# Chunk scan of a gated hybrid block: the preparation of chunk n+1 written ahead of the products of chunk n

## The chip, the cores and the metric

The kernel runs on one core of one Trainium2 chip. Its metric is the device time of one execution in microseconds (us). Three executions of the kernel before took 2009.08, 2011.65 and 2013.90 us; the median is 2011.65 us. The core has a matrix engine (TensorE, PE in the profile, with its weight loads as PEld), a vector engine (DVE), an activation engine (ACT), GpSimd (POOL) and SyncE (SP), which here issues nearly all DMAs. Each engine works off its own instructions in the order in which they stand in the program, and waits at an instruction whose operands are not ready.

## The reference, cut to what matters

The program is one layer of a token mixer with three branches (an S5 scan, a Mamba-2 scan, an RG-LRU), merged by gates, and then an expert-choice mixture of experts. The change lies in the Mamba-2 branch. The sequence of 1024 tokens is cut into 8 chunks of 128; there are 4 groups of 4 heads each, and both directions are computed:

```
a_cum  = cumsum(a)                                   # per chunk and head
cb     = einsum('bcqgn,bcsgn->bgcqs', cm, bm)        # C times B, within a chunk
lmat   = exp(segsum(a))                              # decays within a chunk
y_diag = einsum('bgjcqs,bcsgjp->bcqgjp', cb * lmat, xs)
y_off  = einsum('bcqgn,bcgjpn->bcqgjp', cm, entering) * exp(a_cum)
y      = (y_diag + y_off + D * x) * silu(z)
```

`entering` is the state that enters a chunk; it is there before this stage begins.

## The kernel before, in words

The scan stage treats 32 chunks, group g (0 to 3) by chunk c (0 to 7); "chunk (1,0)" below is group 1, chunk 0, and tiles carry both digits (`rowb10`). `chunk(g, c)` does this for one of them:

- three loads issued by SP: `xe` (inputs and entering states, L790), `bc` (B and C, L792) and `rowb` (decay exponents of 4 heads in 2 directions, 128x1024, L795). Each of the three has 3 buffers, so a load for chunk n+3 waits until chunk n's tile has been read for the last time;
- the decays: ACT makes `dec = exp(rowb)` (two instructions of 64x512, L798; `dec` has 2 buffers); PE multiplies B by C into `pcb` (L800); DVE subtracts and clips `rowb` in place (L802, L803, 128x1024 each), ACT takes the exponential (L804), DVE adds the two directions (L805) and multiplies by `pcb` (L806). POOL multiplies `dec` by C (L807). What is ready for PE at the end is `rowb` by L806 and `dec` by L807;
- the products: 16 small matmuls on PE (L816 with `rowb`, L817 with `dec`) into two PSUM banks `yps`, which collect four chunks;
- after chunks 3 and 7 of a group, DVE adds D*x and multiplies by the gate z (L826, L827), ACT squares (L829, L831), POOL sums the squares (L832), and the result goes out (L833).

Two other works are woven into the same stretch. The RG-LRU branch, four tiles by two directions, has gate products on PE (`lps`, L887), tanh, exp and square root on ACT (L888 to L895) and products and scans on DVE (L894 to L908); a list, `LST`, says after which chunk a piece of it is written. And 24 tasks `gt` project the merge gates: 48 matmuls of 128x512 each on PE (L263 to L265), with a weight split (ACT L125, DVE L126) and an evacuation on ACT (L781). The gate tasks depend on nothing in the scan; they stand behind it in the program.

A scheduler sets the order on each engine from the order in which the program is written and from its own model of durations, so that gate matmuls fill in between the products of the chunks. `bank` gives one of 5 PSUM banks, used by `pcb`, `yps` and `lps` alike. Square root and the exponential are in different activation tables, so that ACT reloads a table before and after each L895.

The loop of the stage calls `chunk(g, c)` for all 32, with pieces of the RG-LRU and of the z projection between them.

Of the kernel before, what the change touches and what calls it, by code (L numbers as in the profile page):

```python
# [62 lines left out]
def backbone(ctx: ExitStack, tc: tile.TileContext, I, out, dbg=None, stop=None):  # L63
# [19 lines left out]
    def bank(name):  # L83
        return bankh[0](name)
# [599 lines left out]
    with tc.tile_pool(name="p2", bufs=1, reuse_waits="tile") as p2:  # L684
# [85 lines left out]
        def z_task(t):  # L770
            def ev(ps, t0, n):
                zt = zp.tile([P, 512], F32, tag="zt", name=f"zt{t}{t0}", bufs=3)
                A.activation(zt, ps, AF.Tanh, scale=0.5)
                V.scalar_tensor_tensor(zt, zt, 1.0, ps, op0=ALU.add, op1=ALU.mult)
                Y.dma_start(szd[t // 2][:, t % 2, t0:t0 + n], zt)
            proj(OFF_Z + t * P, P, False, f"z{t}", ev)
# [7 lines left out]

        yps = {}

        def chunk(g, c):
            q0 = c * P
            xe = p2.tile([P, 512], F32, tag="xe", name=f"xe{g}{c}", bufs=3)
            Y.dma_start(xe, xed[c][:, g, :])  # L790
# [3 lines left out]
            rowb = p2.tile([P, 2, 4, P], F32, tag="rowb", name=f"rowb{g}{c}", bufs=3)  # L794
            Y.dma_start(rowb.rearrange("p d h q -> p (d h q)"), dap(rowsd, (8 * g + c) * 8 * P, [[0, P], [1, 8 * P]]))  # L795
            dec = p2.tile([P, 4, P], F32, tag="dec", name=f"dec{g}{c}", bufs=2)
# [8 lines left out]
            V.tensor_add(rowb[:, 0], rowb[:, 0], rowb[:, 1])  # L805
            V.tensor_mul(rowb[:, 0], rowb[:, 0], pcb[:, None, 0:P].to_broadcast([P, 4, P]))  # L806
            G.tensor_mul(dec, dec, Cd[:, None, :].to_broadcast([P, 4, P]))  # L807
            if c % 4 == 0:
                for t in range(2):
                    yps[t] = bank(f"yps{g}{c}{t}")  # L810
# [100 lines left out]

        zs = [lambda t=t: z_task(t) for t in range(2, 8)]
        lrus = (s_ for t in range(4) for s_ in lru_tile(t))
        for g in range(4):
            for c in range(8):
                chunk(g, c)
                if c in (1, 4) and zs:
                    zs.pop(0)()
                for _ in range(LST[8 * g + c]):
                    next(lrus, None)  # L920
# [661 lines left out]
def build(inputs, dbg=None, stop=None):  # L1582
    import numpy as np
    import concourse.bacc as bacc
    nc = bacc.Bacc("TRN2", target_bir_lowering=False, num_devices=1)
    arrays, I = {}, {}
    for name in _INS:
        a = np.ascontiguousarray(inputs[name])
        arrays[f"in_{name}_dram"] = a
        I[name] = nc.dram_tensor(f"in_{name}_dram", a.shape, mybir.dt.from_np(a.dtype), kind="ExternalInput").ap()  # L1590
    out = nc.dram_tensor("out_0_dram", (1, S, D), F32, kind="ExternalOutput").ap()
    with tile.TileContext(nc, schedule_with_timeline_sim=True) as tc:
        backbone(tc, I, out, dbg=dbg, stop=stop)
    return nc, arrays
# [7 lines left out]
```

## Time and profile before

| what | value |
|---|---|
| profiled execution | 2013.96 us |
| its span on the core | 2012.2 us, so 1.8 us lie around it |
| median of three other runs | 2011.65 us (2009.08 to 2013.90) |
| PE busy over the span | 1873.0 us, 93% |
| DVE busy | 1586.2 us, 79% |
| ACT busy | 1020.2 us, 51% |
| POOL busy | 497.3 us, 25% |
| products of the chunks | from 647.3 to 958 us of the span |

The span has stages with different limits. The scan of the chunks is the stretch from 647.3 to 958 us; behind it PE goes on with the rest of the gate tasks, then with the output projections of the branches and the experts. A time in the profile is counted from the start of the span. The windows of the first group of rows below are cut where the products of chunks (0,0), (1,0), (2,0), (3,0) and (3,7) begin. "Idle before" in a row is the time in which the engine stood still just before the instructions of that row; the name behind the arrow is what ended it, and "issue" stands where the profile names nobody.

### The profile page before, as it was taken

What the parts mean: (1) busy time and instruction counts of PE and PEld (TensorE: products, weight loads), DVE (VectorE), ACT (ScalarE), POOL (GpSimd) and SP (SyncE); (2) the same over time, 40 slices, a digit from 0 to 9 for tenths busy, and PEclk for the clock granted to TensorE, in tenths of its full rate; (3) what the DMA queues carried; (4) which work ended last, traced back from release to release, by engine and by line L of the source; (5) the groups of instructions that cost most, each with busy time, mean ns of one, the idle gap of its engine ahead of it and who ended that gap; (6) DMA issues with size and microseconds to landing.
All of it is one profiled execution on the core that took longest, in us unless ns stands there. A gap on an engine that the chain in (4) does not pass through costs nothing.

```text
span 2012.2 us, 26882 instructions
## 1 busy us (share of the span) xinstructions
PE 1873.0 (93%) x9514; PEld 1503.9 (75%) x9514; DVE 1586.2 (79%) x2183; ACT 1020.2 (51%) x1313; POOL 497.3 (25%) x456
## 2 busy tenths in 40 slices
PE   5989999999899999899999999994699999999997
PEld 2668788887667777677887778773588888888885
DVE  4797778777464788888358855599799999999998
ACT  4533434432322766666421222322488878878785
POOL 1463343340143144332000001246201111010142
PEclk8989999999999999999999999997799999999999
DMA  9234334422677666664578853755799999999974
GB/s 328 36 96 116 103 104 117 120 85 83 189 243 213 193 213 213 217 220 155 185 244 315 279 172 131 258 181 188 260 349 405 390 397 391 401 394 392 375 280 166
DMA packets 273127, 462.64 MB, mean 230 GB/s; under 512 B 39968, under 2 KB 167632, under 8 KB 271968
## 3 DMA queue, kind: packets, MB, share of 16 engines
q1 hardware_dynamic: 268672, 445.19, 63.7%
q0 software_dynamic: 4320, 15.73, 3.0%
q8 instruction: 75, 1.23, 0.2%
q14 instruction: 60, 0.49, 0.1%
HBM read 384.44 MB, written 78.51 MB: 230 GB/s over the span
## 4 chain that ended last, share of the span: by engine, by line
PE 57%; DVE 8%; DMA 5%; issue 3%; ACT 2%; SPq 1%; POOL 1%; DVEq 0%; ACTq 0%; POOLq 0%
PE h_w L1482 6%; PE h_w L1483 6%; PE h_w L1484 6%; PE pj_gt L263 3%; PE pj_gt L265 3%; PE pj_gt L264 3%; PE py_w L1482 3%; PE py_w L1484 3%; PE py_w L1483 3%; PE wo L1299 2%; PE st L754 2%; DMA wm<-in_w_mod_dram 2%; PE bom L264 1%; PE bom L263 1%; PE bom L265 1%
## 5 line engine op out<-in xcount | busy, mean ns | idle before, releaser
L1377 DVE TENSOR_TENSOR el_w<-er_w,eh_w 128x1024 fp32r<-128x1024 f32 x384 | 460.0, 1221 | 25.2 <-ACT eh_w L1376 12.1
L1376 ACT CAST eh_w<-er_w 128x1024 fp32r<-128x1024 f32 x384 | 403.5, 1052 | 106.4 <-PE h_w L1483 66.3
L1482 PE MATMUL h_w<-eh_w,thi_x 128*128 128x512 f32 x512 | 203.5, 397 | 0.0
L1483 PE MATMUL h_w<-eh_w,tlo_x 128*128 128x512 f32 x512 | 200.6, 392 | 0.0
L1484 PE MATMUL h_w<-el_w,thi_x 128*128 128x512 f32 x512 | 200.5, 392 | 0.0
L265 PE MATMUL pj_gt<-hxh,wlo_gt 128*128 128x512 f32 x384 | 153.3, 399 | 0.0
L263 PE MATMUL pj_gt<-hxh,whi_gt 128*128 128x512 f32 x384 | 152.7, 398 | 0.0
L264 PE MATMUL pj_gt<-hxl,whi_gt 128*128 128x512 f32 x384 | 152.6, 397 | 0.0
L1484 PEld LDWEIGHTS h_w<-el_w,thi_x 128*128 128x128 f32 x512 | 96.6, 189 | 20.8 <-DVE el_w L1377 0.2
L1482 PEld LDWEIGHTS h_w<-eh_w,thi_x 128*128 128x128 f32 x512 | 96.7, 189 | 19.6 <-ACT thi_x L1400 0.2
L1483 PEld LDWEIGHTS h_w<-eh_w,tlo_x 128*128 128x128 f32 x512 | 96.7, 189 | 19.6 <-DVE tlo_x L1401 0.4
L1385 POOL DMA_INDIRECT xs<-h2d,idx x16 | 24.0, 1498 | 294.8 <-PE tb_x L1393 273.8
L1482 PE MATMUL py_w<-eh_w,thi_h 128*128 128x512 f32 x240 | 96.4, 402 | 0.0
L1483 PE MATMUL py_w<-eh_w,tlo_h 128*128 128x512 f32 x240 | 93.9, 391 | 0.0
L1484 PE MATMUL py_w<-el_w,thi_h 128*128 128x512 f32 x240 | 93.9, 391 | 0.0
L1418 POOL DMA_INDIRECT accd<-ysm,idx x14 | 49.6, 3545 | 149.5 <-DVE ysm L1416 138.9
L265 PEld LDWEIGHTS pj_gt<-hxh,wlo_gt 128*128 128x128 f32 x384 | 73.3, 191 | 16.8 <-issue 0.8
L263 PEld LDWEIGHTS pj_gt<-hxh,whi_gt 128*128 128x128 f32 x384 | 73.6, 192 | 16.2 <-issue 0.3
L264 PEld LDWEIGHTS pj_gt<-hxl,whi_gt 128*128 128x128 f32 x384 | 73.3, 191 | 16.0 <-issue 0.2
L807 POOL TENSOR_TENSOR dec<-dec,bc 128x512 f32<-128x512 f32 x32 | 61.8, 1935 | 88.8 <-ACT dec L798 88.7
L1207 POOL TENSOR_TENSOR r_wo<-r_wo,bc_m 128x1024 f32<-128x1024 f32 x4 | 10.2, 2558 | 272.4 <-DMA mgm<-mgd 139.4
L265 PE MATMUL pj_xb<-hxh,wlo_xb 128*128 128x512 f32 x192 | 76.8, 400 | 0.5 <-DVE wlo_xb L126 0.5
(650 smaller groups left out, 5013.0 us busy)
## 6 DMA issues: line engine op xcount, KB each, us to landing
er_w<-in_moe_w_dram SPq DMA_DIRECT2D x384, 512.0 KB
rowb<-rowsd SPq DMA_DIRECT2D x32, 512.0 KB
wm<-in_w_mod_dram SPq DMA_DIRECT2D x32, 512.0 KB
raw_gt<-in_w_in_dram SPq DMA_DIRECT2D x24, 512.0 KB
gtd<-gz SPq DMA_DIRECT2D x48, 256.0 KB
xk<-xed SPq DMA_DIRECT2D x18, 512.0 KB
wm<-in_w_mod_dram SPq DMA_DIRECT2D x8, 1024.0 KB
xe<-xed SPq DMA_DIRECT2D x32, 256.0 KB
```

The lines of the kernel that those rows point to most:

```text
L263: T.matmul(ps, wh(k), xh(k), start=(first and k == 0), stop=False)
L264: T.matmul(ps, wh(k), xl(k), start=False, stop=False)
L265: T.matmul(ps, wl(k), xh(k), start=False, stop=(last and k == nk - 1))
L754: T.matmul(st[g // 2][64 * d:64 * d + 64, (g % 2) * 256:(g % 2 + 1) * 256], xk[:, D + 64 * g:D + 64 * g + 64], xd[:, 256 * g:256 * g + 256 ...
L807: G.tensor_mul(dec, dec, Cd[:, None, :].to_broadcast([P, 4, P]))
L1299: T.matmul(st4[i]["ps"][n], ms[i][a][:, k], wo[k][b][:, sl], start=(k == 0 and q == 0), stop=(k == KC - 1 and q == 2))
L1376: A.copy(a, raw)
L1377: V.tensor_sub(b, raw, a.bitcast(F32))
L1418: G.indirect_dma_start(out=accd[:, :], out_offset=bass.IndirectOffsetOnAxis(ap=idx[:, e:e + 1], axis=0), in_=yss[e], in_offset=None, compu ...
L1482: T.matmul(ps[n], xa[:, j, :], a[:, sl], start=(j == 0), stop=False)
L1483: T.matmul(ps[n], xb[:, j, :], a[:, sl], start=False, stop=False)
L1484: T.matmul(ps[n], xa[:, j, :], b[:, sl], start=False, stop=(j == KC - 1))
```

## The change

`chunk(g, c)` is cut in two. `prep(g, c)` holds the loads, the decays and the product of B and C, up to L807, and returns the three tiles. `fin(g, c, ...)` holds the products and what follows them. The loop calls `prep` of the next chunk and then `fin` of the present one; `prep(0, 0)` stands ahead of the loop. No instruction is added or removed, and no buffer count changes.

```
-        def chunk(g, c):
+        def prep(g, c):
             q0 = c * P
             xe = p2.tile([P, 512], F32, tag="xe", name=f"xe{g}{c}", bufs=3)
...
             G.tensor_mul(dec, dec, Cd[:, None, :].to_broadcast([P, 4, P]))
+            return xe, rowb, dec
+
+        def fin(g, c, xe, rowb, dec):
             if c % 4 == 0:
...
+        nxt = prep(0, 0)
         for g in range(4):
             for c in range(8):
-                chunk(g, c)
+                cur, nxt = nxt, (prep(*divmod(8 * g + c + 1, 8)) if 8 * g + c < 31 else None)
+                fin(g, c, *cur)
```

Lines of the new program from `fin` on have numbers higher by 3 (L816 becomes L819, L887 becomes L890, and so on). What the scheduler makes of it is shown at three places; names are those of the tiles, with the two digits of group and chunk (or, for the RG-LRU, the tile `lq1`).

On DVE, between the end of the preparation of chunk (1,7) and that of chunk (2,0), before:

```order
L806 TENSOR_TENSOR rowb17_5846<-rowb17_5846,pcb17_5851 128x512
L903 SCALAR_TENSOR_TENSOR lq1_5828<-la1_5827,li1_5744 128x256
L802 TENSOR_TENSOR rowb20_5884<-rowb20_5884,XL_4507 128x1024
L904 SCALAR_TENSOR_TENSOR lq1_5828<-la1_5827,lq1_5828,li1_5744 128x1024
L803 TENSOR_TENSOR rowb20_5884<-rowb20_5884,lim_4511 128x1024
L905 TENSOR_TENSOR lh1_5650<-lh1_5650,lq1_5828 128x1024
L826 SCALAR_TENSOR_TENSOR xq17_5867<-xq17_5867,Dc_4547,yps140_5669 128x512
L805 TENSOR_TENSOR rowb20_5884<-rowb20_5884 128x512
L826 SCALAR_TENSOR_TENSOR xq17_5867<-xq17_5867,Dc_4547,yps141_5670 128x512
L827 TENSOR_TENSOR xq17_5867<-xq17_5867,zq17_5869 128x512
L908 SCALAR_TENSOR_TENSOR lh1_5650<-lh1_5650,la1_5827 128x1024
L806 TENSOR_TENSOR rowb20_5884<-rowb20_5884,pcb20_5889 128x512
```

and the last twelve of the instructions between the same two now; ahead of them, behind L806 of `rowb17`, stand L899 of `li1`, L802 of `rowb20`, L900 of `li1` and L803 of `rowb20`:

```order
L829 SCALAR_TENSOR_TENSOR xq17_5884<-xq17_5884,Dc_4547,yps140_5686 128x512
L906 SCALAR_TENSOR_TENSOR lq1_5845<-la1_5844,li1_5761 128x256
L829 SCALAR_TENSOR_TENSOR xq17_5884<-xq17_5884,Dc_4547,yps141_5687 128x512
L802 TENSOR_TENSOR rowb21_5901<-rowb21_5901,XL_4507 128x1024
L830 TENSOR_TENSOR xq17_5884<-xq17_5884,zq17_5886 128x512
L907 SCALAR_TENSOR_TENSOR lq1_5845<-la1_5844,lq1_5845,li1_5761 128x1024
L805 TENSOR_TENSOR rowb20_5863<-rowb20_5863 128x512
L830 TENSOR_TENSOR xq17_5884<-xq17_5884,zq17_5886 128x512
L803 TENSOR_TENSOR rowb21_5901<-rowb21_5901,lim_4511 128x1024
L908 TENSOR_TENSOR lh1_5667<-lh1_5667,lq1_5845 128x1024
L126 TENSOR_TENSOR wlo_gt12_7336<-raw_gt12_7333,whi_gt12_7335 128x1024
L806 TENSOR_TENSOR rowb20_5863<-rowb20_5863,pcb20_5868 128x512
```

Between the two L806 stood 10 other instructions and now stand 15, among them the first two of chunk (2,1), while the old L896 and L897 of the RG-LRU have moved here from ahead of chunk (1,7).

On PE, behind the products of chunk (1,0), before:

```order
L817 MATMUL yps101_5426<-dec10_5414,xe10_5408 64x128
L887 MATMUL lps1000_5458<-lxh1_5447,lwh1_5443 128x512
L887 MATMUL lps1000_5458<-lxl1_5448,lwh1_5443 128x512
L887 MATMUL lps1000_5458<-lxh1_5447,lwl1_5444 128x512
L887 MATMUL lps100512_5463<-lxh1_5447,lwh1_5443 128x512
L887 MATMUL lps100512_5463<-lxl1_5448,lwh1_5443 128x512
L887 MATMUL lps100512_5463<-lxh1_5447,lwl1_5444 128x512
L887 MATMUL lps1001027_5468<-lxe1_5449,lwh1_5443 128x256 x2
L887 MATMUL lps1001027_5468<-lxe1_5449,lwl1_5444 128x256
L263 MATMUL pj_gt04_512_6995<-hxh6_372,whi_gt04_6963 128x512
L264 MATMUL pj_gt04_512_6995<-hxl6_380,whi_gt04_6963 128x512
L265 MATMUL pj_gt04_512_6995<-hxh6_372,wlo_gt04_6964 128x512
```

and now:

```order
L820 MATMUL yps101_5443<-dec10_5394,xe10_5388 64x128
L890 MATMUL lps1000_5475<-lxh1_5464,lwh1_5460 128x512
L890 MATMUL lps1000_5475<-lxl1_5465,lwh1_5460 128x512
L890 MATMUL lps1000_5475<-lxh1_5464,lwl1_5461 128x512
L890 MATMUL lps100512_5480<-lxh1_5464,lwh1_5460 128x512
L890 MATMUL lps100512_5480<-lxl1_5465,lwh1_5460 128x512
L890 MATMUL lps100512_5480<-lxh1_5464,lwl1_5461 128x512
L890 MATMUL lps1001027_5485<-lxe1_5466,lwh1_5460 128x256 x2
L890 MATMUL lps1001027_5485<-lxe1_5466,lwl1_5461 128x256
L819 MATMUL yps100_5442<-rowb11_5429,xe11_5425 64x128
L820 MATMUL yps100_5442<-dec11_5431,xe11_5425 64x128
```

The products of chunk (1,1) now follow at once, where gate matmuls stood; those have moved ahead of chunk (1,0). Over a whole group, chunks 0 and 1, 2 and 3, 4 and 5 now stand close together (before: 1 and 2, 3 and 4).

On ACT, around the square root of RG-LRU tile 1, before:

```order
L888 ACTIVATE li1_5744<-lps111512_5792,lbh_4943 128x512
L798 ACTIVATE dec17_5848<-rowb17_5846 64x512 x2
L895 ACT_TABLE_LOAD
L895 ACTIVATE lq1_5828<-lq1_5828 128x1283
L868 CAST lwh2_5915<-lw2_5909 128x512
L888 ACT_TABLE_LOAD
L888 ACTIVATE li1_5744<-lps1111027_5797,lbh_4943 128x256
L125 CAST whi_gt11_7273<-raw_gt11_7271 128x1024
L781 ACTIVATE gz07512_7206<-pj_gt07_512_7181 128x512
L804 ACTIVATE rowb17_5846<-rowb17_5846 128x1024
L798 ACTIVATE dec20_5886<-rowb20_5884 64x512 x2
```

and now:

```order
L891 ACTIVATE li1_5761<-lps111512_5809,lbh_4943 128x512
L804 ACTIVATE rowb17_5823<-rowb17_5823 128x1024
L125 CAST whi_gt11_7273<-raw_gt11_7271 128x1024
L781 ACTIVATE gz07512_7206<-pj_gt07_512_7181 128x512
L898 ACT_TABLE_LOAD
L898 ACTIVATE lq1_5845<-lq1_5845 128x1283
L871 CAST lwh2_5932<-lw2_5926 128x512
L891 ACT_TABLE_LOAD
L891 ACTIVATE li1_5761<-lps1111027_5814,lbh_4943 128x256
L798 ACTIVATE dec20_5865<-rowb20_5863 64x512 x2
L781 ACTIVATE gz100_7240<-pj_gt10_0_7215 128x512
```

The exponential of chunk (1,7) has moved ahead of the square root with its two table loads, and the last piece of `li1` (the old L888, on which the old L896 of DVE waits) has moved behind three more instructions.

## Rows read from the trace of the kernel before

**Rows 1.** Windows by group: length; busy PE, PEld, DVE, ACT, POOL; PEclk; DMA share; GB/s.
```profile
647.30:728.20 80.90, 76.15 (x411) 59.75 (x410) 64.60 (x55) 51.40 (x67) 26.47 (x17) 0.96 0.60 187
728.20:806.30 78.10, 75.60 (x412) 59.13 (x412) 64.83 (x57) 54.65 (x70) 30.77 (x20) 0.98 0.71 221
806.30:888.60 82.30, 74.56 (x400) 57.78 (x400) 69.22 (x57) 53.81 (x69) 30.44 (x19) 0.96 0.65 208
888.60:957.50 68.90, 65.05 (x356) 50.84 (x355) 57.80 (x49) 46.16 (x58) 20.74 (x12) 0.95 0.57 184
```

**Rows 2.** Groups by line, PE, 640 to 960 us (busy, mean ns | idle before).
```profile
L816 PE MATMUL yps<-rowb,xe 128*64 128x128 f32 x256 | 29.5, 297 | 17.2 <-issue 15.4 <-ACT rowb L804 1.3 <-ACT lr L893 0.2
```

**Rows 3.** Timeline of PE, the longest gap of the stage (start, duration, [idle before]).
```profile
716.71 0.70 PE L816 MATMUL yps<-rowb,xe 128*64 128x128 f32 x4 [3.98 <-issue]
```

**Rows 4.** Timeline of DVE around that gap.
```profile
715.96 0.65 DVE L806 TENSOR_TENSOR rowb<-rowb,pcb 128x512 f32<-128x512 f32 x1
716.54 2.72 DVE L802 TENSOR_TENSOR rowb<-rowb,XL 128x1024 f32<-128x1024 f32 x1
```

**Rows 5.** Chain of waits behind that gap (start, time in the chain).
```profile
720.29 0.43 PE pj_gt L263
...
728.30 0.38 PE yps L816 x4
...
729.38 1.96 PE lps L887 x9
731.33 0.23 PE pj_gt L263
```

**Rows 6.** Groups by line and shape, DVE, 650 to 960 us.
```profile
L803 DVE TENSOR_TENSOR rowb<-rowb,lim 128x1024 f32<-128x1024 f32 x30 | 56.2, 1875 | 0.5
L802 DVE TENSOR_TENSOR rowb<-rowb,XL 128x1024 f32<-128x1024 f32 x30 | 45.5, 1517 | 31.6 <-ACT dec L798 31.6
L126 DVE TENSOR_TENSOR wlo_gt<-raw_gt,whi_gt 128x1024 fp32r<-128x1024 f32 x17 | 23.2, 1363 | 1.8 <-ACT whi_gt L125 1.5 <-DMA bc<-bcd 0.2
L805 DVE TENSOR_TENSOR rowb<-rowb 128x512 f32<-128x512 f32 x30 | 21.4, 715 | 7.9 <-ACT rowb L804 7.8
L806 DVE TENSOR_TENSOR rowb<-rowb,pcb 128x512 f32<-128x512 f32 x31 | 21.0, 678 | 6.1 <-PE pcb L800 4.9
L896 DVE SCALAR_TENSOR_TENSOR li<-li,lxc 128x1283 f32<-128x1283 f32 x8 | 16.3, 2034 | 1.5 <-ACT li L888 1.5
L904 DVE TENSOR_TENSOR_SCAN lq<-la,lq,li 128x1024 f32<-128x1024 f32 x4 | 12.5, 3127 | 0.0
L897 DVE SCALAR_TENSOR_TENSOR li<-lq,li 128x1283 f32<-128x1283 f32 x8 | 11.9, 1482 | 0.0
L827 DVE TENSOR_TENSOR xq<-xq,zq 128x512 f32<-128x512 f32 x14 | 10.6, 789 | 0.0
L826 DVE SCALAR_TENSOR_TENSOR xq<-xq,Dc,yps 128x512 f32<-128x512 f32 x14 | 9.8, 737 | 0.0
L905 DVE TENSOR_TENSOR lh<-lh,lq 128x1024 f32<-128x1024 f32 x4 | 5.8, 1438 | 0.0
L903 DVE TENSOR_TENSOR_SCAN lq<-la,li 128x256 f32<-128x256 f32 x4 | 3.4, 839 | 0.0
```

**Rows 7.** Source line L803: count, durations in ns min/median/max.
```profile
L803 DVE TENSOR_TENSOR rowb<-rowb,lim x32: 1208/2186/3340, 561.9 to 949.2; 128x1024 f32<-128x1024 f32 x32
```

**Rows 8.** Groups by line and shape, POOL, 650 to 960 us.
```profile
L807 POOL TENSOR_TENSOR dec<-dec,bc 128x512 f32<-128x512 f32 x30 | 58.6, 1957 | 85.2 <-ACT dec L798 85.1
```

**Rows 9.** Timeline of ACT at one square root.
```profile
741.85 1.28 ACT L895 ACT_TABLE_LOAD   x1
743.14 1.28 ACT L895 ACTIVATE lq<-lq 128x1283 f32<-128x1283 f32 x1
...
749.30 1.27 ACT L798 ACTIVATE dec<-rowb 64x512 f32<-64x512 f32 x2 [1.23 <-DMA rowb<-rowsd]
```

**Rows 10.** Timeline of SP: issue of the load that ended this wait.
```profile
742.78 0.32 SPq L795 DMA_DIRECT2D rowb<-rowsd  x1
```

## The prediction, made before the changed kernel was run

> **What bounds the kernel now.** I read the windows first, cut by group of chunks. From the first product of chunk (0,0) to that of chunk (3,7) PE is busy for 76.15 + 75.60 + 74.56 + 65.05 = 291.4 of 310.2 us, DVE for 256.5, ACT for 206.0 [rows 1]. PE is nearest to its limit, and the gate matmuls that fill it have to be done whatever the order; so the stage can only give back what PE stands still or runs slowly, and the reader is to look for that. Next come PE's groups by line: 17.2 us of idle time stand ahead of the chunk products L816 [rows 2], nearly all of the 310.2 - 291.4 = 18.8 us. The timeline shows the longest, 3.98 us, ended at 716.71 [rows 3] and put down to "issue". The timeline of DVE tells more: L806 of the same chunk ends at 715.96 + 0.65 = 716.61, 0.1 us earlier [rows 4]. PE has arrived at the product before DVE has made its operand. The chain then shows gate matmuls 0.43 us apart behind the gap and 0.23 us later on [rows 5]: the clock has fallen to its 1.2 GHz level and come back to 2.4. The granted shares 0.96, 0.98, 0.96 and 0.95 cost at most 80.9 x 0.04 + 78.1 x 0.02 + 82.3 x 0.04 + 68.9 x 0.05 = 11.5 us [rows 1]. Idle time and slow clock together are 28.7 us, the most that any order can give back here.
>
> Behind the stage PE goes on with gate tasks, so time saved or lost on PE before chunk (3,7) is handed on.
>
> **The change, part by part.** It removes and adds no instruction, DMA, table load or buffer. What moves is the order, on all five queues. A scheduler that knew the true durations would leave PE no gap; the one that made the old order did not, and made the new one too. So I lay the durations of the trace along the new order.
>
> *The run from chunk 7 to the next chunk 0* is the worst place, three times (into groups 1, 2 and 3). On PE stand now 67 gate matmuls (counted in the order), 67 x 0.23 = 15.4 us, the products of chunk 7, 729.38 - 728.30 = 1.1 us [rows 5], and two B-C products, at 0.2 each as an estimate from the 0.23 of a gate matmul: 16.9 us. On DVE stand 16 instructions from behind L806 of chunk 7 up to L806 of chunk 0. By their means [rows 6]: L896 2.03, two L802 3.03, L897 1.48, two L803 3.75, two L826 1.47, L903 0.84, two L827 1.58, L904 3.13, L805 0.72, L905 1.44, L126 1.36, L806 0.68, together 21.5 us. One instruction starts 0.07 us before the end of the one ahead (716.61 against 716.54 [rows 4]), so 16 x 0.07 = 1.1 comes off: 20.4 us. Besides, L896 has to wait for the last piece of `li1`. Between the exponential of chunk 7 and that piece ACT now has two table loads and a square root, 3 x 1.28 = 3.8 us [rows 9], and four shorter ones; no row here has them, and I estimate them at 0.7 each like the 0.68 of a 128x512 on DVE [rows 6]: 6.6 us. DVE fills 0.72 + 1.36 + 0.68 - 0.2 = 2.6 of that, so it waits about 4 (bounds: none, if ACT is ahead, and 6.6, if DVE fills nothing). DVE needs 24.4 us where PE needs 16.9.
>
> *Its lead at chunk 7* comes off. The three `rowb` buffers bound it: the load for chunk 7 goes out when chunk 4's products are done, lands 749.30 - 742.78 = 6.5 us later [rows 9, 10], and 1.3 for the exponential, 3.4 for L802 and L803, 1.1 for L804 (an estimate from twice the elements of L798's half), and 1.4 for L805 and L806 make 13.7 us. PE takes 1.96 + 1.1 + 39 x 0.23 + 1.96 + 1.1 + 17 x 0.23 = 19.0 us from there to chunk 7 [rows 5] (matmuls counted in the order). Of the 5.3 between, the 3.4 of chunk 6's L802 and L803 come off: a lead of 2 us. Chunk 0 is then late by 24.4 - 16.9 - 2 = 5.5 us, three times 16.5 us. If idle time costs slow clock as now, 11.5 / 17.2 = 0.67 for each us, that is another 11.0. PE's account: 27.5 against 28.7 us, a gain of 1.2.
>
> *The whole group, along DVE.* This checks it, since PE's slow matmuls lie beside DVE's catching up. DVE has about 67 us of work in a group of eight ((64.8 + 69.2) / 2 of groups 1 and 2 [rows 1]). It waits 4 us at L896; twice about 4 at an L802 whose `rowb` load goes out only behind products that now stand close in front (chunks 3 and 7; today all such waits are 31.6 us in the stage, 8 a group [rows 6]); and about 4 where the split of a gate weight and `dec` of chunk 4 stand behind the other two table loads on ACT. That is 83 us. Three groups make 249 us and carry 713 gate matmuls; today they take 241.3 [rows 1] and carry 679 (both counted in the order), so 34 x 0.23 = 7.8 us of later work is done: even. The last group has no chunk behind it and no such run; to the start of chunk (3,7) I come to 60 us with 167 gate matmuls against 68.9 with 183, and less 16 x 0.23 = 3.7 that is a gain of 5.
>
> Of 1 and 5 us I take 4, nearer to the second, because DVE is what the products wait for. Profiled execution against profiled execution: 2013.96 - 4 = 2009.96 us. The median shown is 2.3 us under that execution, so the time to predict is 2011.65 - 4 = 2007.65, rounded to 2007.5 us.
>
> **Two rules of the Trainium skill.** L803 takes 1.21 us at least, 2.19 in the median and 3.34 at most [rows 7], with POOL's L807, 1.96 us each [rows 8], started by the same `dec`. The Trainium skill, "SBUF — State Buffer", section Who interferes with whom, says that a DVE instruction with two inputs in SBUF contends with a GpSimd instruction that reads SBUF, and that the one that starts first holds the shared ports for its whole length. The trace agrees: 3.34 is near 1.21 + 1.96. It speaks against this change, in that two chunks' L802 and L803 stand in one run; the fourth rival below works that out from rows. The other: table load and square root follow each other without a gap, 741.85 + 1.28 = 743.13 against 743.14 [rows 9]. The Trainium skill, "ScalarE: Activation LUTs", section What ACT_TABLE_LOAD costs, has 1.28 us for the load and another 1.38 us of drain for each switch. By it L896 would wait 2.8 us longer three times, 8 us in all, and my gain would turn into a loss; these rows show no drain, and the sum goes by them.
>
> **The rivals.** (1) My forecast: gaps go at most chunks and come back at each chunk 0; 2007.5 us, its own range 2003.5 to 2011. (2) ACT runs ahead, and L896 doesn't wait. For it: today this wait is 1.5 us in eight [rows 6]. Against it: the piece of `li1` now stands behind more. Chunk 0 is late by 1.5 instead of 5.5, so 12 us of idle time and 0.67 x 12 = 8 of clock go: 20 less, some of which DVE's other waits take back; half of it gives 2011.65 - 4 - 10 = 1997.5. (3) The waits only move: as much idle time and slow clock as now, with DVE as the true bound in both orders; 2011.65. For it: the two accounts lie within 5 us of that. (4) Slower: in the run from chunk 7 to chunk 0 DVE loses its ports to POOL, since L802 and L803 of two chunks and both their L807 fall into it. With both L803 at 3.34 instead of 1.88 us [rows 6, 7] a run grows by 2.9; three make 8.8, so 2011.65 - 4 + 8.8 = 2016.5, and more if the run from chunk 3 to 4 grows too (up to 2020). It decides when the lateness at chunk 0 is over 8 us. For it: those means are of an order in which such runs were shorter. Against it: POOL is busy for 108 of 310 us in both [rows 1]. That the change does nothing is out: the order differs on every engine.
>
> **How the numbers follow.** About 0.2%, 4 us, is what a measurement of this kernel can tell from no change. Chances: (1) 0.36, (2) 0.16, (3) 0.26, (4) 0.22. The forecast lies at the edge of that bound, so it goes to faster and same: 0.27 and 0.09. With (2), faster has 0.27 + 0.16 = 0.43; the third goes to same but for 0.03 on either side, 0.20, so that faster is 0.46 and same 0.29; slower is 0.22 + 0.03 = 0.25. The range 1996 to 2018 leaves out 1 in 10 on each side: below it lies (2) with most of its 20 us, above it (4) with the second run.
>
> **What would show it.** In the new profile, DVE's L806 ends 0.1 us ahead of the first product of chunks (1,0), (2,0) and (3,0) with a gap of 4 to 7 us each, and other gaps are under 2; DVE's L896 waits for ACT's `li`, 3 to 4 us at these places. From chunk 0 to chunk 0 a group takes 82 to 85 us. More than 87 speaks for (4), less than 80 for (2). No gap over 2 us at any chunk 0 would show my account of DVE wrong; a stage that is shorter while the end is not would show that time isn't handed on.

## The result and the profile after

The changed kernel takes 2022.1 us in the median of 4 runs (2015.83 to 2022.90), the kernel before on the same chip 2011.63 us; the ratio is 1.0052 with a 95% interval of 1.004 to 1.0064. It is slower by about 10.5 us; 2007.5 was forecast. Profiled execution against profiled execution it is 2021.31 against 2013.96 us.

The windows, cut where the products of chunks (0,0), (1,0), (2,0), (3,0) and (3,7) begin, answer to [rows 1]; columns as there.

```profile
647.50:727.90 80.40, 74.44 (x415) 58.87 (x415) 65.66 (x56) 53.59 (x69) 27.71 (x18) 0.99 0.61 194
727.90:817.30 89.40, 81.19 (x422) 63.93 (x423) 70.34 (x58) 54.90 (x70) 31.35 (x20) 0.94 0.61 198
817.30:906.30 89.00, 80.58 (x422) 63.27 (x423) 70.31 (x58) 54.68 (x70) 31.07 (x19) 0.94 0.60 196
906.30:972.60 66.30, 62.83 (x335) 49.16 (x335) 48.82 (x43) 44.86 (x55) 17.92 (x10) 0.92 0.58 180
sum 325.10, PE 299.03 PEld 235.22 DVE 255.12 ACT 208.03 POOL 108.04; mean PE 74.76 PEld 58.81 DVE 63.78 ACT 52.01 POOL 27.01
```

The stage is 325.1 us long and was 310.2. The trace counts 880 gate matmuls in it and 862 before; 18 times 0.23 us is work that the end is spared, so the stage lost 14.9 - 4.1 = 10.8 us, near the 10.5 of the medians. In the two profiled executions all of it is still there where the gate tasks end (1035.6 against 1024.8 us), but only 7.3 us at the end of the span: 3.5 come back behind the gate tasks, where the kernel before stands still for 2.60 us at L1019 and the changed one for 0.6. PE stands still for 325.1 - 299.0 = 26.1 us (18.8 before), and the granted shares cost 80.4 x 0.01 + 89.4 x 0.06 + 89.0 x 0.06 + 66.3 x 0.08 = 16.8 us (11.5 before). DVE is busy for 255.1 us against 256.5: over the stage it has nothing more to do, it waits more.

PE's groups by line, 640 to 975 us, answer to [rows 2]: the chunk products have the same idle time as before (now 14.3 us of it at the three chunks 0 and 2.8 at three chunks 4), and 8.9 us have come up at L890, gate products of the RG-LRU, where there was none.

```profile
L819 PE MATMUL yps<-rowb,xe 128*64 128x128 f32 x256 | 30.7, 310 | 17.1 <-issue 14.3 <-ACT whi_gt L125 2.8
L890 PE MATMUL lps<-lxe,lwh 128*128 128x256 f32 x32 | 7.6, 323 | 8.9 <-DVE rowb L806 8.9
```

The timeline of PE at chunk (1,0) and ahead of chunk (1,5) shows one gap of each kind [rows 3]:

```profile
727.89 0.70 PE L819 MATMUL yps<-rowb,xe 128*64 128x128 f32 x4 [5.96 <-issue]
...
774.43 0.77 PE L890 MATMUL lps<-lxe,lwh 128*128 128x256 f32 x2 [2.98 <-DVE rowb L806]
774.99 0.42 PE L890 MATMUL lps<-lxe,lwl 128*128 128x256 f32 x1
775.34 0.70 PE L819 MATMUL yps<-rowb,xe 128*64 128x128 f32 x4
```

The timeline of DVE at the same places [rows 4]:

```profile
725.98 1.21 DVE L126 TENSOR_TENSOR wlo_gt<-raw_gt,whi_gt 128x1024 fp32r<-128x1024 f32 x1
727.11 0.67 DVE L806 TENSOR_TENSOR rowb<-rowb,pcb 128x512 f32<-128x512 f32 x1
...
768.56 2.34 DVE L904 TENSOR_TENSOR_SCAN lh<-la,lq,li 128x1024 f32<-128x1024 f32 x1
770.82 0.66 DVE L805 TENSOR_TENSOR rowb<-rowb 128x512 f32<-128x512 f32 x1
771.40 2.28 DVE L126 TENSOR_TENSOR wlo_gt<-raw_gt,whi_gt 128x1024 fp32r<-128x1024 f32 x1
773.61 0.68 DVE L806 TENSOR_TENSOR rowb<-rowb,pcb 128x512 f32<-128x512 f32 x1
```

L806 of chunk (1,0) ends at 727.78, 0.1 us ahead of the product, as forecast. The L806 that ends at 774.29 is that of chunk (1,5). L890 waits for it because a B-C product holds the PSUM bank it is to get; but the products of that chunk stand 0.9 us behind it and need the same L806. So the bank mostly stands for another wait: without it PE would stand still at L819, for all but those 0.9 us.

DVE's groups, 650 to 975 us, answer to [rows 6]:

```profile
L803 DVE TENSOR_TENSOR rowb<-rowb,lim 128x1024 f32<-128x1024 f32 x30 | 54.3, 1809 | 0.6
L802 DVE TENSOR_TENSOR rowb<-rowb,XL 128x1024 f32<-128x1024 f32 x30 | 39.9, 1330 | 43.1 <-ACT dec L798 38.2 <-PE pcb L800 4.8
L126 DVE TENSOR_TENSOR wlo_gt<-raw_gt,whi_gt 128x1024 fp32r<-128x1024 f32 x18 | 25.1, 1397 | 10.3 <-ACT whi_gt L125 8.4 <-PE lps L890 2.0
L805 DVE TENSOR_TENSOR rowb<-rowb 128x512 f32<-128x512 f32 x30 | 22.4, 747 | 0.0
L806 DVE TENSOR_TENSOR rowb<-rowb,pcb 128x512 f32<-128x512 f32 x30 | 20.4, 679 | 3.9 <-PE pcb L800 2.6
L830 DVE TENSOR_TENSOR xq<-xq,zq 128x512 f32<-128x512 f32 x14 | 19.4, 1388 | 0.0
L899 DVE SCALAR_TENSOR_TENSOR li<-li,lxc 128x1283 f32<-128x1283 f32 x8 | 13.7, 1710 | 11.1 <-ACT li L891 11.1
```

The idle column is the one to read. L805 and L806 no longer wait for the chunk's own exponential or B-C product (14.0 us before, 3.9 now): that is what an early preparation bought. In exchange the waits at L802 grew from 31.6 to 43.1, at L126 from 1.8 to 10.3 and at L899 from 1.5 to 11.1, most of them ended by ACT: 29.6 us more for 10.1 less. At L126 and L899 it is ACT's own queue that comes late. At L802 ACT for the most part passes a wait on: `dec` has to read `rowb` before L802 overwrites it, and ACT itself stands still ahead of `dec` until the load of `rowb` has landed. ACT's row of before (650 to 960 us), the same row now (650 to 975 us), and ACT and DVE at chunk (1,3), one of the two longest of these waits:

```profile
L798 ACT ACTIVATE dec<-rowb 64x512 f32<-64x512 f32 x58 | 36.4, 627 | 15.7 <-DMA rowb<-rowsd 8.8 <-issue 4.7 <-POOL lr L881 1.5
L798 ACT ACTIVATE dec<-rowb 64x512 f32<-64x512 f32 x58 | 36.4, 628 | 40.9 <-issue 18.5 <-DMA rowb<-rowsd 16.9 <-PE pj_gt L264 2.7
...
738.68 1.27 ACT L798 ACTIVATE dec<-rowb 64x512 f32<-64x512 f32 x2 [3.36 <-DMA rowb<-rowsd]
739.99 1.23 DVE L802 TENSOR_TENSOR rowb<-rowb,XL 128x1024 f32<-128x1024 f32 x1 [5.28 <-ACT dec L798]
```

That load went out at 729.97, just behind the products of chunk (1,0), whose buffer it takes. By the windows DVE stands still for 325.1 - 255.1 = 70.0 us of the stage, and stood for 310.2 - 256.5 = 53.7.

### The profile page after: what moved, and what is told of

Its sections match the earlier page's. It is cut to its first block, busy times and chain, and to the rows that moved or that the text cites. A ratio compares the mean times of both kernels' runs of the same rounds, so it can differ in the third digit from the quotient of the medians.

```text
span 2019.5 us, 26893 instructions
## 1 busy us (share of the span) xinstructions
PE 1874.4 (93%) x9514; PEld 1507.5 (75%) x9514; DVE 1592.4 (79%) x2183; ACT 1021.4 (51%) x1313; POOL 502.3 (25%) x456
## 5 line engine op out<-in xcount | busy, mean ns | idle before, releaser
L807 POOL TENSOR_TENSOR dec<-dec,bc 128x512 f32<-128x512 f32 x32 | 65.6, 2054 | 117.5 <-ACT dec L798 106.2
L802 DVE TENSOR_TENSOR rowb<-rowb,XL 128x1024 f32<-128x1024 f32 x32 | 45.1, 1410 | 43.1 <-ACT dec L798 38.2
```

The source lines that it names most:

```text
L802: V.tensor_sub(rowb, rowb, XL[:, c, :, 4 * g:4 * g + 4][:, :, :, None].to_broadcast(sh))
```

## The experiments

All were timed beside the kernel before; the ratio is to it, and "against before" is the ratio times its median. "Stage" is the stretch of the products from chunk (0,0) to (3,7) in the profiled execution, less 0.23 us for each gate matmul in it; "idle" is PE's in that stretch, its length less PE's busy time in the windows.

| kernel | median us | ratio, 95% interval | against before | stage | idle |
|---|---|---|---|---|---|
| before | 2011.6 | | | 112.0 | 18.8 |
| changed | 2022.1 | 1.0052, 1.0040 to 1.0064 | +10.5 | 122.7 | 26.1 |
| e1 | 2009.6 | 0.9997, 0.9985 to 1.0008 | -0.6 | 111.7 | 18.7 |
| e2 | 2012.8 | 1.0007, 0.9997 to 1.0018 | +1.4 | 113.1 | 20.3 |
| e3 | 2006.5 | 0.9977, 0.9966 to 0.9987 | -4.6 | 107.3 | 16.5 |
| e4 | 2002.0 | 0.9948, 0.9933 to 0.9963 | -10.5 | 103.2 | 14.1 |
| e5 | 1994.2 | 0.9925, 0.9913 to 0.9938 | -15.1 | 90.7 | 6.2 |
| e6 | 2000.0 | 0.9955, 0.9942 to 0.9968 | -9.0 | 101.3 | 12.7 |
| e7 | 2023.8 | 1.0066, 1.0050 to 1.0081 | +13.3 | 122.5 | 28.8 |
| e8 | 1995.1 | 0.9928, 0.9916 to 0.9941 | -14.5 | 95.8 | 10.6 |
| e9 | 2013.3 | 1.0005, 0.9995 to 1.0015 | +1.0 | 111.0 | 19.0 |
| e10 | 2002.9 | 0.9954, 0.9940 to 0.9969 | -9.3 | 106.9 | 17.9 |
| e11 | 2011.3 | 0.9996, 0.9987 to 1.0005 | -0.8 | 111.8 | 19.3 |
| e12 | 1998.2 | 0.9933, 0.9920 to 0.9945 | -13.5 | 94.0 | 6.8 |
| e13 | 2001.8 | 0.9948, 0.9936 to 0.9960 | -10.5 | 103.2 | 14.8 |
| e14 | 1995.6 | 0.9929, 0.9916 to 0.9941 | -14.3 | 95.7 | 11.1 |
| e15 | 2012.0 | 1.0006, 0.9997 to 1.0015 | +1.2 | 110.2 | 20.1 |
| e16 | 2002.5 | 0.9957, 0.9945 to 0.9969 | -8.6 | 100.3 | 15.0 |
| e17 | 1995.1 | 0.9924, 0.9910 to 0.9938 | -15.3 | 98.4 | 10.6 |
| e18 | 1987.8 | 0.9894, 0.9875 to 0.9912 | -21.3 | 87.9 | 3.4 |

**Which part of the move acts (e1, e2, e7, e9).** In e1 the B-C product and L805, L806 go back behind the move:

```
-            pcb = bank(...); T.matmul(pcb...)     # in prep
-            V.tensor_add(...); V.tensor_mul(...)  # L805, L806
+            (the same four lines at the head of fin)
```

> The changed kernel with one part undone: the B-C product and the two DVE instructions behind it (L805, L806) stand with the chunk's own products again; loads, both exponentials, subtraction, clip and POOL's product stay one chunk ahead. Theory A, the place of the B-C product alone is what the change acts through, and loads and decays one chunk earlier in the text are without effect: the time of before, 2011.6 us (within 4), stage from chunk (0,0) to (3,7) 310 us. Rival B, the early loads and decays are what costs, through a longer DVE run ahead of chunk 0: 2018 to 2022 us, with the gaps of 4 to 6 us ahead of chunks (1,0), (2,0), (3,0).

2009.6 us. On all five engines the order is, names aside, that of the kernel before, instruction by instruction: loads and decays one chunk earlier in the text change nothing by themselves. Rival B, in which they cost, falls.

e2 does the other half alone, in the kernel before: `ahead(g, c)` holds the load of B and C and the B-C product, and the loop calls it one chunk early.

> The kernel before with one part done: only the load of B and C and the B-C product stand one chunk ahead; the other loads and all decays stay in place. Theory A: the time of the changed kernel, 2022 us (2018 to 2026), gaps of 4 to 6 us ahead of three chunks 0 and of about 3 us near three chunks 5. Rival B: the time of before, 2011.6 us (within 4).

2012.8 us: theory A falls as well. PE's groups show the pattern of the changed kernel, gaps ahead of chunks 0 and at L892 (its number for L890), smaller in sum (20.3 us of idle time in the stage for 26.1), though not at each place:

```profile
L821 PE MATMUL yps<-rowb,xe 128*64 128x128 f32 x256 | 30.5, 310 | 12.6 <-issue 11.7 <-DVE rowb L811 0.9
L892 PE MATMUL lps<-lxe,lwh 128*128 128x256 f32 x32 | 7.2, 308 | 7.7 <-DVE rowb L811 7.7
```

Neither half costs by itself; the whole does. So the question became what the whole preparation is moved past: the products of chunk n, or the RG-LRU pieces that follow them. e7 moves it past the pieces alone:

```
-                cur, nxt = nxt, (prep(...) if ... else None)
-                fin(g, c, *cur)
+                fin(g, c, *nxt)
+                nxt = prep(...) if ... else None
```

> The changed kernel with the preparation of chunk n+1 written behind the products of chunk n, but still ahead of the RG-LRU pieces that follow chunk n. Theory I, what costs is that preparation passes the RG-LRU's gate products and vector work, which then come late in DVE's run ahead of chunk 0: 2018 to 2022 us, gaps of 4 us or more at chunks 0. Rival J, what costs is that it passes the products themselves: 2008 to 2014 us, like before.

2023.8 us, the whole cost and perhaps more. PE's timeline has its four longest gaps ahead of chunks (1,0), (1,7), (3,0) and (3,5), three of them ended by DVE's L806 and one put down to an evacuation on ACT. Only two of the four, at chunks (1,0) and (3,0), lie where the changed kernel's long gaps do:

```profile
716.68 0.49 PE L819 MATMUL yps<-rowb,xe 128*64 128x128 f32 x2 [4.01 <-DVE rowb L806]
...
792.68 0.34 PE L819 MATMUL yps<-rowb,xe 128*64 128x128 f32 x2 [3.37 <-ACT gz L781]
...
883.71 0.49 PE L819 MATMUL yps<-rowb,xe 128*64 128x128 f32 x2 [5.40 <-DVE rowb L806]
...
932.41 0.34 PE L819 MATMUL yps<-rowb,xe 128*64 128x128 f32 x2 [3.08 <-DVE rowb L806]
```

e9 keeps the preparation ahead of the products and writes the pieces ahead of both:

```
+        for _ in range(LST[0]):
+            next(lrus, None)
...
-                for _ in range(LST[8 * g + c]):
+                for _ in range((LST + (0,))[8 * g + c + 1]):
```

> The changed kernel with the RG-LRU pieces of each chunk written ahead of the preparation that the change moved past them (pieces of chunk n, then preparation of n+1, then products of n), so that preparation still passes the products but no longer those pieces. Theory I, passing the RG-LRU pieces is the cost: 2006 to 2014 us. Rival K, an early preparation costs whatever it passes: 2018 to 2026 us.

2013.3 us: the cost is gone but for 1.0 us (interval -1.0 to +3.0). Theory I holds for these texts: a whole preparation that passes the products is harmless, one that passes the RG-LRU pieces costs 10 to 13 us. The pieces of the z projection, which stand between the chunks too, are passed in e9 as well and so are not the cause. In e2, e7 and e9 the scheduler makes the order of all engines anew, so that they compare whole orders.

**Banks and load buffers (e3 to e6, e8, e12).** e4 and e5 give the B-C products one bank of their own, e3 and e6 a fourth `rowb` buffer, e8 and e12 both; e3, e4, e8 in the changed kernel, e5, e6, e12 in the kernel before:

```
+        pcbt = bank("pcbt")
-            pcb = bank(f"pcb{g}{c}")
+            pcb = pcbt[:, (c % 4) * P:(c % 4 + 1) * P]
...
-            rowb = p2.tile(..., tag="rowb", ..., bufs=3)
+            rowb = p2.tile(..., tag="rowb", ..., bufs=4)
```

> The changed kernel with 4 buffers of rowb for 3, nothing else. Theory C, the groups last 89 us because DVE waits at L802 for loads that can go out only when products standing close together are done (waits of 5.3, 1.8 and 3.6 us in each of the middle groups): most of those 10.7 us a group go, 3 groups, about 20 us with some taken back by other waits: 2002 to 2010 us. Rival D, DVE's run ahead of chunk 0 sets the groups, and loads are hidden or their waits only move: within 4 us of 2022.

> The changed kernel with the B-C products of all chunks in four quarters of one PSUM bank that they keep, so that 4 banks are left to yps and lps and no lps waits for a bank that a B-C product holds. Theory E, the three stalls of 2.98 us of PE at L890, and the slow clock behind them, are a price of their own: they go, 3 times 2.98 + about 2 us of slow clock, 15 us: 2005 to 2009 us. Rival F, PE would wait there for DVE's L806 anyway, since the products of the chunk of that L806 stand right behind the lps: gaps of about 3 us at L819 of chunks 5 in their place, within 4 us of 2022.

> The kernel before (nothing moved ahead) with the B-C products in four quarters of one PSUM bank of their own. Theory G, the early preparation is good in itself and only the shared banks made it lose: this kernel stays near 2011 us (2007 to 2013), 5 us or more above the changed kernel with the same bank (2002.0). Rival H, the bank of its own is the gain, and with it the order of the text matters little: 1999 to 2005 us, within 3 of the changed kernel with that bank.

> The kernel before with 4 buffers of rowb for 3. Theory G, the early preparation needs the fourth buffer and gains by it, the old order does not: 2009 to 2012 us. Rival H, the fourth buffer is a gain by itself, whatever the order: 2003 to 2008 us, within 3 of the changed kernel with 4 buffers (2006.5).

> The changed kernel with both: the B-C products in a bank of their own and 4 buffers of rowb. If banks and load buffers were two limits of their own, the gains over the changed kernel (2022 to 2002.0 and 2022 to 2006.5) add up in part: 1992 to 1999 us. If both relieve the same wait, DVE's, there is little behind the first: 2000 to 2005 us.

> The kernel before with the B-C products in a bank of their own and 4 buffers of rowb. If the two gains (2011 to 1994.2 and 2011 to 2000.0) add up: 1983 to 1989 us. If they relieve the same wait: 1990 to 1996 us. By rival K it lies 5 us or more below the changed kernel with both (1995.1).

By themselves e3 (2006.5) and e4 (2002.0) seemed to bear out theories C and E. The controls say otherwise: the kernel before gains by the bank and by the buffer too (15.1 and 9.0 us, where the changed one gains 21.0 and 15.1) and ends lower (1994.2 and 2000.0). So H is nearer than G: both edits are good in themselves. But both times lie below H's ranges, and with either edit the changed order is 4.6 and 4.4 us behind the old one and not within 3. With both edits the two orders are equal (-14.5 and -13.5, intervals overlap): e8 came where two limits of their own would have put it, e12 in neither of its two ranges and not 5 us below e8, so rival K falls; e12 is no better than e5, so the gains don't add up there. The cost of the change thus goes from 10.5 us to 4.5 with either edit and to nothing with both: it hangs on the shared banks and on the three load buffers. In these six kernels, too, the scheduler makes its order anew, so that none of them compares one order with one wait more or less. e5 is, with e8 inside its interval, the fastest kernel of those that compute everything: 15.1 us under the kernel before, with PE idle for 6.2 us in its stage:

```profile
642.70:940.60 297.90, 291.66 (x1608) 229.33 (x1607) 253.86 (x214) 208.17 (x266) 109.20 (x67) 0.99 0.67 211
```

**Through which engine (e10, e11, e13 to e18).** e10 and e11 leave out the clip L803 in the kernel before and in the changed one:

```
-            V.tensor_tensor(rowb, rowb, lim..., op=ALU.min)
-            A.activation(rowb, rowb, AF.Exp)
+            A.activation(rowb, rowb, AF.Exp, scale=0.0)
```

> The kernel before without the clip L803 (left out, with the exponential behind it taken of zero times its input): DVE has 32 times about 1.85 us less, some 15 us a group. It is the base for the next run. Where DVE is what the products wait for, the stage gets shorter: 1990 to 2003 us. Where PE is the bound, within 5 us of 2011.

> The changed kernel without the clip L803, left out as in the run before this one. Theory L, the change costs through DVE, whose groups of 89 us get longer by what is put late in the runs ahead of chunks 0 and 4: with 15 us less work a group that is covered, and this kernel lies within 4 us of the kernel before without the clip. Rival M, the cost is in PE's order or in ACT, and doesn't hang on DVE's load: 7 to 13 us above the kernel before without the clip.

The changed kernel stays 8.5 us behind, in M's range. Theory L falls as it was put: a lighter DVE doesn't cover the cost. But here too the order was made anew, with fewer gate matmuls in the stage (688 for 880), so PE came as early as DVE did.

The four runs after that hold the order fixed: replacing the square root by a hyperbolic tangent (L898, e13 and e14), or the eight long scans by a multiply and add (L904, L907, e15 and e16), leaves every engine's order as it was, but for the table loads. e17 and e18 do both.

```
-                A.activation(q, q, AF.Sqrt)
+                A.activation(q, q, AF.Tanh)
...
-                    V.tensor_tensor_scan(hs, a[:, 0:S], ig[:, 0:S], q[:, 1282:1283], ...)
+                    V.scalar_tensor_tensor(hs, a[:, 0:S], q[:, 1282:1283], ig[:, 0:S], ...)
```

> The changed kernel with the square root of the RG-LRU replaced by a hyperbolic tangent, which stands in the same table as the exponential, so that 16 table loads of 1.28 us go and the order of all engines stays. Theory N, ACT carries the cost: li and the dec behind the square root come 2.6 us earlier six times, DVE's waits of 2.6 to 3.6 us at L899 shrink, 8 to 13 us in all: 2009 to 2014 us, and 0 to 5 above the kernel before with the same edit. Theory L, DVE's own work carries it: within 4 of 2018 us, 7 to 11 above that one.

> The kernel before with the same edit (hyperbolic tangent for square root, 16 table loads less, same order), the base for the run before. ACT is on DVE's path at few places here (waits of 1.2 to 1.5 us): 2005 to 2010 us.

> The changed kernel with the RG-LRU's eight long scans on DVE replaced by a multiply and add of the same size, same order; an estimate from L897 (1.49 us for 1283) is 1.2 us in place of 2.4 to 2.6. Theory L, DVE's runs ahead of chunks 0 and 4 carry the cost: the gaps at six places shrink by 1.2 us each, with slow clock 8 to 10 us: 2012 to 2014 us, and 2 to 6 above the kernel before with this edit. Theory N, ACT: L899 and L802 then wait longer, 2018 to 2021 us, 8 to 12 above that one.

> The kernel before with the same edit (multiply and add for the eight long scans), the base for the run before. Its gaps lie at chunks 1 to 6 of a group and only part of them behind a scan: 2005 to 2010 us.

e13, e14 and e16 gained more than any theory had said; e15 came at the time that theory L gave it, but 9.8 us above its control, where N had put it. In the changed kernel 16 table loads of 1.28 us, 20.5 us of ACT, were worth 10.5 + 10.5 = 21.0 us, and the scans, which got 8.5 us shorter in all (20.3 to 11.8), 10.5 - 1.2 = 9.3. In the kernel before the same edits gave 14.3 and 8.6. ACT is busy for 1021.4 of 2019.5 us, 51%, and yet a microsecond off it or off DVE is 0.7 to 1.1 us off the kernel: what the stage waits for is the path through both. Not all of that is waiting. PE's idle time fell by 11.3 and 7.7 us without the table loads and by 6.0 and 3.8 with the short scans; the rest goes with the slow clock, whose granted share over the stage was 0.95 and 0.96 and is 0.97 to 0.99 with these edits. PE's rows of e13 (640 to 956 us) and of e15 (640 to 960 us) show which gaps went:

```profile
L819 PE MATMUL yps<-rowb,xe 128*64 128x128 f32 x256 | 29.2, 298 | 12.8 <-issue 12.8
L890 PE MATMUL lps<-lxe,lwh 128*128 128x256 f32 x32 | 7.1, 306 | 2.0 <-DVE rowb L806 2.0
...
L819 PE MATMUL yps<-rowb,xe 128*64 128x128 f32 x256 | 30.1, 306 | 17.9 <-issue 17.2 <-ACT whi_gt L125 0.7
L890 PE MATMUL lps<-lxe,lwh 128*128 128x256 f32 x32 | 7.1, 304 | 2.2 <-DVE rowb L806 2.2
```

The gaps at chunks 4 and 5, 2.8 + 8.9 = 11.7 us in the changed kernel, are down to 2.0 and 2.9; those at the three chunks 0, 14.3 us, are 12.8 and 17.2. DVE's groups of e13, 650 to 956 us, show which waits of DVE went:

```profile
L802 DVE TENSOR_TENSOR rowb<-rowb,XL 128x1024 f32<-128x1024 f32 x30 | 44.4, 1480 | 38.5 <-ACT dec L798 38.5
L126 DVE TENSOR_TENSOR wlo_gt<-raw_gt,whi_gt 128x1024 fp32r<-128x1024 f32 x18 | 21.9, 1217 | 5.9 <-ACT whi_gt L125 5.7 <-PE yps L820 0.2
L899 DVE SCALAR_TENSOR_TENSOR li<-li,lxc 128x1283 f32<-128x1283 f32 x8 | 16.0, 1997 | 2.6 <-ACT li L891 2.6
```

L899 waits 2.6 us instead of 11.1, L126 5.9 instead of 10.3, L802 38.5 instead of 43.1: 17.5 us. The place is seen on ACT ahead of chunk (1,0), in the changed kernel:

```profile
700.71 1.28 ACT L898 ACT_TABLE_LOAD   x1
702.00 1.28 ACT L898 ACTIVATE lq<-lq 128x1283 f32<-128x1283 f32 x1
703.18 0.60 ACT L871 CAST lwh<-lw 128x512 fp32r<-128x512 f32 x1
703.80 1.28 ACT L891 ACT_TABLE_LOAD   x1
705.10 0.48 ACT L891 ACTIVATE li<-lps,lbh 128x256 f32<-128x256 f32 x1
705.47 1.26 ACT L798 ACTIVATE dec<-rowb 64x512 f32<-64x512 f32 x2
```

and in e13:

```profile
701.12 1.27 ACT L898 ACTIVATE lq<-lq 128x1283 f32<-128x1283 f32 x1
702.28 0.62 ACT L871 CAST lwh<-lw 128x512 fp32r<-128x512 f32 x1
702.79 0.49 ACT L891 ACTIVATE li<-lps,lbh 128x256 f32<-128x256 f32 x1
703.16 1.28 ACT L798 ACTIVATE dec<-rowb 64x512 f32<-64x512 f32 x2
```

`li` and `dec` come 2.3 us earlier. The difference between the two orders is 21.0 - 14.3 = 6.7 us smaller without the table loads, 3.8 us of 10.5 (the two intervals leave some 3.5 us either way), and 0.7 smaller with short scans, 9.8. Of N and L, then, N has the larger part, though the edit on ACT is also the larger one (20.5 us against 8.5).

> The changed kernel with both edits of the four runs before: hyperbolic tangent for the square root (16 table loads less) and multiply and add for the eight long scans; order as in the changed kernel. Theory O, the change lengthens the path through ACT and DVE that both orders wait for, and what is left is covered as the path gets shorter: 1991 to 1996 us, and 0 to 4 above the kernel before with both edits. Rival P, a part of the cost stands at chunk 0 and is not covered by a shorter path, since gaps of 3 to 5 us were left there with one edit: 1995 to 2000 us, and 5 to 9 above that one.

> The kernel before with the same two edits, order as before. Idle time and slow clock were 29.6 us in its stage, 12.7 with the table loads gone and 17.4 with the scans shortened, so little can be left: 1987 to 1993 us.

With both edits 6.0 us are left, 7 by the medians. That is rival P's range, but the two intervals leave 4.7 us either way, so that the times alone don't exclude theory O. PE's timeline in e17 shows where they are, at chunks (2,0) and (3,0):

```profile
805.73 0.49 PE L819 MATMUL yps<-rowb,xe 128*64 128x128 f32 x2 [3.63 <-issue]
...
887.65 0.48 PE L819 MATMUL yps<-rowb,xe 128*64 128x128 f32 x2 [3.30 <-issue]
```

The windows of the whole stage, e17 first and then e18, columns as above:

```profile
647.60:948.40 300.80, 290.20 (x1589) 229.27 (x1588) 250.41 (x212) 186.85 (x248) 104.76 (x67) 0.98 0.64 208
```

```profile
647.90:934.10 286.20, 282.80 (x1575) 221.40 (x1574) 250.67 (x215) 184.85 (x248) 105.60 (x67) 0.99 0.69 217
```

The old order has almost no idle time left there (3.4 of 286.2 us); the new one has 10.6, most of it (1.8, 3.6 and 3.3) ahead of the three chunks 0. At chunks 4 and 5 it is nearly gone.

**What is shown and what is open.** Shown: the cost arises when the whole preparation passes the RG-LRU pieces, hardly with less, and not where the B-C products have a bank and `rowb` a fourth buffer; both orders wait for the path through ACT and DVE; the new one lets DVE wait longer for ACT and, through it, for loads; its gaps at chunks 4 and 5 go with the table loads or the long scans, and it keeps gaps at chunks 0 that a shorter path doesn't cover. Not shown: that passing the pieces costs in any order, since each text was tried in the one order that the scheduler made of it, and e7 loses in part at other places than the changed kernel. Open: how the 10 us divide between the waits for ACT and the length of DVE's run ahead of chunk 0, since with one of the two lightened the other took over; and why the cost vanishes with a bank and a buffer more.

## Why the prediction was wrong

**What held.** PE's product comes 0.1 us behind L806 at each chunk 0 with gaps of 6.0, 4.1 and 4.3 us, 14.3 in all, where 5.5 three times was forecast. DVE waits for `li` there, 2.6 to 3.6 us for a forecast 4. The run from L806 of chunk (1,7), which ends at 791.43, to the end of that of (2,0) at 817.16 is 25.7 us against 24.4, with a shorter wait and longer instructions than forecast (see rival 4), so that its nearness is in part luck. What the stage lost was handed on to the end of the gate tasks, and 7.3 of the 10.8 us to the end of the span.

**Rival 4** fails on its own row: L803 takes 1.81 us in the mean, against 1.88, and no more than 2.31 against 3.34 [rows 7]:

```profile
L803 DVE TENSOR_TENSOR rowb<-rowb,lim x32: 1211/1946/2307, 561.7 to 958.6; 128x1024 f32<-128x1024 f32 x32
```

The prediction had read the 3.34 us as L803 beside L807; in the trace before, that L803 (from 796.58) stands beside another POOL instruction, the split `lxl` of the RG-LRU (from 794.61, 4.23 us). But the cost that rival 4 had in mind came in other instructions. In the three runs to a chunk 0 the 16 DVE instructions take 23.3, 24.3 and 24.3 us in all, where their means of before make 21.5, and each that is 0.4 us or more above its mean lies beside a POOL instruction. The longest is L830, here ahead of chunk (1,0):

```profile
715.99 2.88 DVE L830 TENSOR_TENSOR xq<-xq,zq 128x512 f32<-128x512 f32 x1
715.20 3.12 POOL L877 TENSOR_TENSOR lxl<-lxc,lxh 128x1024 fp32r<-128x1024 f32 x1 [3.25 <-ACT lxh L876]
```

That is 2.5 us a run for the rival's 2.9. Its condition, a lateness over 8 us at chunk 0, was not met (6.0, 4.1 and 4.3). So "more than 87 speaks for (4)", met by 89.4 and 89.0 us a group, points to a part of the loss and not to the whole of it.

**The step that failed** is the sum on PE's account, "27.5 against 28.7 us, a gain of 1.2". It took chunk 0 for the one late place and set all other gaps at nothing ("other gaps are under 2"). The trace has 2.8 us at chunks 4 and 8.9 at L890 ahead of chunks 5, so 26.1 us of idle time for 16.5. From L806 of chunk (1,4) to that of chunk (1,5) DVE needs 774.29 - 768.64 = 5.65 us, for the scan L904, L805, a split of 2.28 us and L806, where PE has 2.7 us of work behind the start of chunk (1,4), at 768.74. Slow clock is 16.8 for 11.0: at 16.8 / 26.1 = 0.64 for each us idle the price of 0.67 was good for this kernel, and what it was applied to was short. (It is no fixed price: e7 has 28.8 us of idle time and 305.1 x 0.04 = 12.2 of slow clock, 0.42 for each.) Together 42.9 us against 18.8 + 11.5 = 30.3 are a loss of 12.6 us, near the 10.8 of the stage (a share is given to 0.01, 3 us over the stage). The late place had been seen: the account along DVE speaks of 4 us where the split of a gate weight and `dec` of chunk 4 stand behind the other two table loads. It was entered in DVE's account and left out of PE's. The run to chunks 4 and 5 is of the same make as that to chunk 0: a square root with two table loads on ACT, then a scan, a split and L806 on DVE. With the order held, taking out the table loads or shortening the scans removes 9.7 or 8.8 us of these 11.7 (e13, e15).

**The account along DVE** failed too, by less: 83 us a group were forecast; 80.4 came for the first and 89.4 and 89.0 for the next two. DVE's work is 70.3 us in a group and not 67: 58 instructions stand in it for 57, and four L830 at 1.39 us for 0.79 are 2.4 us of it. Its waits are 89.4 - 70.3 = 19.1 us, not 16. Three groups of 249 us would have been even; 258.8 are not. The last group took 66.3 us with its 167 gate matmuls where 60 were forecast: against 68.9 us and 183 that is 2.6 - 3.7 = -1.1, no gain in place of the 5 on which the forecast leaned.

**Of the two rules of the Trainium skill**, the one on ports, "SBUF — State Buffer", section Who interferes with whom, is borne out: of the 30 L803 of the stage the 20 that take over 1.3 us all lie beside a POOL instruction, and 19 of 19 did before. But the new order moves the collisions to other instructions more than it adds any: L830 takes 1.39 us in the mean (0.79 before, as L827 [rows 6]), L802 1.33 (1.52 before), and DVE's busy time over the stage stays the same. On the table load the runs are plainer than the rows were. The Trainium skill, "ScalarE: Activation LUTs", section What ACT_TABLE_LOAD costs, adds 1.38 us of drain to each 1.28; by that, 16 loads would be worth an estimated 42.6 us on ACT, by the rows 20.5. The traces show no drain: ACT stands still for 0.02 us at most ahead of each of the 16 loads in the stage and 0.01 behind it (once 0.30, in the kernel before). And `li`, which starts 705.10 - 700.71 = 4.39 us after the first of two loads, starts 702.79 - 701.12 = 1.67 us after the activation in its place in e13: 1.36 us less for each load, and not 2.66. So the sum was right to leave the drain out. The 21.0 and 14.3 us of the kernels don't decide this by themselves, since a part of them is clock.

## What to carry to other kernels

In this kernel, work written earlier was harmless where it passed work of its own chain, and cost 10 to 13 us where it passed another chain that feeds the same in-order engines, as long as banks and load buffers were short: ask of a moved block what it is put ahead of, not only what it is put ahead for, and what it has to share there. When idle time is forecast engine by engine, carry every late place from one engine's account into the other's; a place that is in one sum only is a term lost. An engine that is busy for half the span can still set the time: look for the waits that name it on the next engine (here ACT on DVE), then for what it waits for itself (here at `dec` a load), and test by shortening one instruction with the order held fixed.

## What the runs showed of the hardware that was not expected

An edit of one kind of ACT instruction was worth more than any move of the text: 16 table loads of 1.28 us, 1% of the span, were 14.3 and 21.0 us of the kernel's time, about half of it as idle time of PE (7.7 and 11.3 us) and the rest with its slow clock. A fourth load buffer gave 9.0 us and a PSUM bank that the B-C products keep gave 15.1 us to the kernel before, and the two together 13.5, not more than the better one, each with an order made anew.
